# One more step ahead of the recurrence's output products, a copy moved to ScalarE, and four output stores for five

## The chip, the cores and the metric

The kernel runs on one core of one Trainium2 chip. The metric is the device time of one execution in microseconds (us). Weights, activations and output lie in the chip's HBM; one launch computes the whole layer.

## What is computed

One layer of a hybrid decoder trunk on 256 tokens of width 2048, in float32. The combined projection feeds a short convolution (branch A), a gated linear recurrence with eight heads (branch B) and two merge gates; three more projections follow.

```python
h = rmsnorm(x, norm_mix_g[i])
u = h @ w_in[i]                                  # 2048 -> 12288 columns
c_g, b_g, xa, za, q, fl, iv, og, ga, gb = jnp.split(u, split_idx, axis=-1)
ya = b_g * causal_dwconv3(c_g * xa, conv_w[i]) * jax.nn.silu(za)
# branch B, heads of 128, in chunks of the sequence:
#   a  = q . decay . k          (lower triangle of a chunk)
#   o  = (q exp b) @ state + a @ v
o = hgrn2_chunked(silu(q), kk, iv, log_f)
o = o * lax.rsqrt(jnp.mean(o * o, axis=-1, keepdims=True) + EPS)
yb = o * hg_norm_g[i] * jax.nn.silu(og)
m = jax.nn.sigmoid(ga) * (ya @ w_a_out[i]) + jax.nn.sigmoid(gb) * (yb @ w_b_out[i])
x = x + m @ w_o[i]
gate = jax.nn.sigmoid(rmsnorm(x, ple_norm_g[i]) @ w_ple_gate[i])
x = x + gate * (p[i] @ w_ple_proj[i])
return rmsnorm(x, final_norm_g)
```

## The kernel before

The 256 tokens are two tiles of 128 rows (`t` is 0 or 1). All projections run through one loop over `steps`. A step is one 256-row piece of a weight matrix by 512 columns: two row tiles `k` of 128, two token tiles `t`, and three products each, because every float32 operand is held as a rounded part and a remainder (`whi`, `wlo` for weights; `xh`, `xl` and the like for activations). So a step is twelve `L937` matmuls into two PSUM banks `g`. The order of the groups of steps is written out by hand: the projection of `p`, then for each half `j` of the recurrence and convolution columns `f, q, iv, og, c, xa, za, b` with eight steps each, then the gates with the two branch outputs, then `O` and `PG`.

Ahead of the products of a step, `split` makes the weights of the step three further on: ScalarE rounds (`L124`, `whi`), VectorE takes the remainder (`L125`, `wlo`). There are four buffers of each, so a new `whi` starts when TensorE has finished with the step four earlier. `load` asks for the raw weights further ahead still, on SyncE's DMA queue, a pair of steps in one 1 MB transfer (`L103`) into three buffers.

What belongs to a finished group of columns (its epilogue) is a Python generator. After each step, `advance` lets every active generator run to its next `yield`; so a `yield` puts what follows it one step of twelve matmuls later in the program. The engines execute their instructions in program order and wait for one another by semaphores; a scheduler may shift an instruction by a few places.

`hgrn(j)` is the generator of the recurrence for half `j` of the heads, four heads each; it runs twice, under the products of `c, xa, za, b` of the same half. With masked level products it builds the matrix `a` of 128 by 128 for each head and each token tile, and the product `bo` that links the two token tiles. Near its end stand these steps: the products `bo` (`L512`) and `bk` (`L389`); two yields; `bo` is copied from PSUM to `aoff` (`L522`), and pieces of `bk` are copied under a mask into `a[:, 0]` and `a[:, 1]` by `keep` (`L396`, eight instructions); a yield; then the twelve output products `o` (`L529`, `L530`, `L531`), each of 128 by 128 in two passes:

```python
nc.tensor.matmul(o[0][:, hs], a[:, 0, h, :], v[...], start=True, stop=True)      # L529
nc.tensor.matmul(o[1][:, hs], aoff[:, h, :], v[...], start=True, stop=False)     # L530
nc.tensor.matmul(o[1][:, hs], a[:, 1, h, :], v[...], start=False, stop=True)     # L531
```

Behind them come the squares of `o` (`L541`, ScalarE), the gate (`L547`, VectorE), the norm (`L206`, `L210`), the scaling (`L555`, ScalarE), and `turned`: four stores to DRAM (`L233`), one load back (`L235`), both on SyncE's queue, and after three more yields a transposition on VectorE (`L239`), from which `put` makes `ybT` (`L197`, `L198`). The convolution's generators run in the same stretch: `L595` and `L604` are its taps, `L264` and `L272` gates, and `ep_b` turns its own tile the same way, so its `L233` and `L235` stand in the same queue.

At the end, the last group `PG` is worked off in three parts: token tile 0, and the two halves of 256 columns of token tile 1. After each tile `last_norm(t)` gets `r`, the reciprocal root of the mean square (`L759`, `L760`), scales the 2048 columns of the tile in place and stores them. Columns 0 to 1023 are scaled by ScalarE (`L774`), 1024 to 1535 by VectorE (`L776`), 1536 to 2047 by VectorE with the gain (`L770`); each store (`L777`) goes out right after its piece is scaled, on SyncE's queue but for one on ScalarE's.

Of the kernel before, what the change touches and what calls it, by code (L numbers as in the profile page):

```python
# [11 lines left out]
AF = mybir.ActivationFunctionType  # L12
ALU = mybir.AluOpType
# [10 lines left out]
CW = 512  # L24
# [20 lines left out]
def hybrid_kernel(ctx, tc, xT, x, pT, prm, gfin, masks, w_in, w_a, w_b, w_o, w_pg, w_pp, out):  # L45
    nc = tc.nc
# [27 lines left out]
    def nm(s):  # L74
        uid[0] += 1
        return f"{s}_{uid[0]}"
# [5 lines left out]
    def bank(tag):  # L82
        return ps.tile([P, CW], F32, tag=tag, bufs=4, name=nm(tag))

    def sc(n, tag="sc", bufs=12):
        return small.tile([P, n], F32, tag=tag, bufs=bufs, name=nm(tag))
# [130 lines left out]
    def spread(ap, t):  # L217

        return ap.rearrange("p (b c t e) -> p t c b e", b=4, c=4, t=NT)[:, t]
# [120 lines left out]
    def ep_og(j, psum):  # L343
        sg, o = t4(), t4("og", 1)
        sig(psum, sg)
        times(psum, sg, o)
        state["og", j] = o
        yield
        yield from hgrn(j)

    def hgrn(j):
# [21 lines left out]
        aoff = tmp.tile([P, 4, P], F32, tag="aoff", bufs=1, name=nm("aoff"))  # L373

        def heads(ap):
            return ap.rearrange("p (h t) -> p h t", h=4)

        def quarters(B):

            n = max(B // 2, 32)  # L380
            for r in range(P // n):
                c = r ^ 1 if B >= 64 else r
                yield slice(r * n, (r + 1) * n), slice(c * n, (c + 1) * n)
# [10 lines left out]
        def keep(dst, mask, src, B):  # L394
            for r, c in quarters(B):
                nc.vector.copy_predicated(  # L396
                    out=dst[r, :, c], data=src[r, :, c],
                    mask=mask_t[r, mask : mask + 1, c].to_broadcast([r.stop - r.start, 4, c.stop - c.start]),
                )
# [24 lines left out]
        def level(B):  # L424
# [19 lines left out]
            out=y.rearrange("p (n c) -> p n c", c=SCAN), in0=b.rearrange("p (n c) -> p n c", c=SCAN),  # L444
# [11 lines left out]
        for i in range(0, len(LEVELS), 2):  # L456
# [19 lines left out]
            out=el, in0=yl,  # L476
# [12 lines left out]
            out=f.rearrange("p (n c) -> p n c", c=1), in0=br, in1=bl, op=ALU.subtract  # L489
# [8 lines left out]
        for blk in range(2):  # L498
# [4 lines left out]
                out=a[:, blk],  # L503
# [4 lines left out]
        bo = bank("s")  # L508
# [10 lines left out]
            products(bk[blk], lambda h: kk[:, h, :], lambda h: qq[:, h, :], 2)  # L519
        yield  # L520
        yield
        nc.vector.tensor_copy(out=aoff.rearrange("p h t -> p (h t)"), in_=bo)  # L522
        for blk in range(2):
            keep(a[:, blk], len(LEVELS) + 2 + blk, heads(bk[blk]), 2)
        yield
        o = [bank("s") for _ in range(2)]
        for h in range(4):
# [9 lines left out]
        for n in range(8):  # L537
            t, h = n // 4, n % 4
            if n == 4:
                yield  # L540
            nc.scalar.activation(  # L541
                out=sq[:, n * P : (n + 1) * P], in_=o[t][:, h * P : (h + 1) * P], func=AF.Square,
                scale=state["rstd1"][:, t : t + 1], accum_out=ss[:, n : n + 1],
            )
        for t in range(NT):
            s = slice(t * CW, (t + 1) * CW)
# [4 lines left out]
        for n in range(8):  # L551
            t, h = n // 4, n % 4
            if n == 4:
                yield
            nc.scalar.activation(  # L555
                out=spread(sq, t)[:, h], in_=yb[:, n * P : (n + 1) * P].rearrange("p (b e) -> p b e", e=32),
                func=AF.Identity, scale=rh[:, n : n + 1],
# [198 lines left out]
    def last_norm(t):  # L756

        xs, r, tot = state["x"], sc(1, "r3", 2), state["tot3", t]
        nc.vector.tensor_tensor(out=tot, in0=tot, in1=state["ss3"][:, t * 6 + 4 : t * 6 + 5], op=ALU.add)  # L759
        nc.gpsimd.tensor_tensor(out=r, in0=tot, in1=mhalf[:, :1], op=ALU.pow)  # L760
        n = CW // 2

        for eng, q0, q1, queue in (
            (nc.vector, 4, 5, nc.sync), (nc.vector, 5, 6, nc.sync), (nc.scalar, 0, 2, nc.sync),
            (nc.vector, 6, 8, nc.sync), (nc.scalar, 2, 4, nc.scalar),
        ):
            s = slice(q0 * n, q1 * n)
            d = xs[:, t, s]
            if q0 >= 6:
                nc.vector.scalar_tensor_tensor(  # L770
                    out=d, in0=d, scalar=r, in1=state["gfin"][:, s], op0=ALU.mult, op1=ALU.mult
                )
            elif eng is nc.scalar:
                nc.scalar.activation(out=d, in_=d, func=AF.Identity, scale=r)  # L774
            else:
                nc.vector.tensor_scalar(out=d, in0=d, scalar1=r, scalar2=None, op0=ALU.mult)  # L776
            queue.dma_start(out=out[:, t, s], in_=d)  # L777

    def ep_last(t, halves):

        last_half(t, 0, halves[0])
        sums_so_far(t)
        last_half(t, 1, halves[1])
        last_norm(t)
        yield
# [154 lines left out]
    for pos, (gi, c) in enumerate(steps[:last_group]):  # L940
# [36 lines left out]
        for i in range(2):  # L977
            k = 2 * c + i
            s = slice(i * CW, (i + 1) * CW)
# [41 lines left out]
    for t, halves in ((0, (0, 1)), (1, (0,)), (1, (1,))):  # L1021
        bk, n = bank("g"), CW // 2
        for c in range(nlast):
# [4 lines left out]
            for i in range(2):  # L1028
                k = 2 * c + i
                s = slice(i * CW + halves[0] * n, i * CW + (halves[-1] + 1) * n)  # L1030
# [5 lines left out]
        else:  # L1036
            last_half(t, halves[0], bk[:, :n])
            if halves[0] == 0:
                sums_so_far(t)
    last_norm(1)  # L1040
    finish()
    close_pool("tmp3")
# [73 lines left out]
```

## Time and profile before

| what | value |
|---|---|
| time, median of 3 runs | 831.42 us (831.42 to 831.85) |
| the profiled execution's own time | 831.84 us |
| span of the profiled execution, first to last instruction | 830.1 us |
| TensorE matmuls busy | 816.9 us (98%) |
| VectorE busy | 538.3 us (65%) |
| ScalarE busy | 430.9 us (52%) |
| DMA moved | 187.25 MB, mean 226 GB/s |
| granted TensorE clock | 0.996 |

The profile shows one execution. Times in its views are us from the start of the span. A timeline row gives the start, the duration, the engine, the source line, the operation, and the output and input tiles with their shapes; in brackets stands how long the engine sat idle before the row and what ended that. PE is the matmul, PEld the weight load that runs beside it, DVE VectorE, ACT ScalarE, POOL GpSimd, SPq the queue of SyncE and ACTq the queue of ScalarE. Matmuls are pipelined: each is recorded longer than the distance to the next one, so the rate is read from the starts. A row can hold several instructions (x8), and then its duration covers them all. The chain of waits is followed back from the last instruction, at each step to what released it.

### The profile page before, as it was taken

How to read it: one execution, taken by the hardware profiler on the slowest of the kernel's cores; microseconds unless marked ns; L12 is line 12 of the kernel's file. 1: busy time of each engine (PE TensorE's matmuls, PEld its weight loads, DVE VectorE, ACT ScalarE, POOL GpSimd, SP SyncE). 2: the span in 40 equal slices, each digit the busy share in tenths (PEclk: the TensorE clock that was granted, in tenths of full speed). 3: DMA queues.
4: the chain of work that ended last, by engine and by line, in shares of the span. 5: the costliest groups of instructions: out<-in, count | busy, mean ns of one | idle time of the engine just before them, and what ended most of it. 6: DMA issues, size and time to landing. Idle time of an engine off the chain costs nothing.

```text
span 830.1 us, 10589 instructions
## 1 busy us (share of the span) xinstructions
PE 816.9 (98%) x4122; PEld 674.3 (81%) x4122; DVE 538.3 (65%) x662; ACT 430.9 (52%) x553; POOL 84.8 (10%) x74
## 2 busy tenths in 40 slices
PE   9999999999999999999999999999999999999995
PEld 6888888878888888878888888888888888888885
DVE  6746678896866588896745545545645656679633
ACT  7666565446564465455544443443444455566522
POOL 1000035110000054100001001000100000001210
PEclk9999999999999999999999999999999999999998
DMA  9969655647876554657655755755655787987702
GB/s 341 372 256 340 222 193 197 204 153 219 277 235 232 203 203 152 204 192 241 227 203 172 254 189 196 253 203 191 231 191 198 253 281 246 330 304 269 293 0 103
DMA packets 40947, 187.25 MB, mean 226 GB/s; under 512 B 4672, under 2 KB 14400, under 8 KB 22720
## 3 DMA queue, kind: packets, MB, share of 16 engines
q1 hardware_dynamic: 40464, 185.78, 64.7%
q10 hardware_dynamic: 432, 0.79, 0.3%
q8 instruction: 32, 0.52, 0.3%
q14 instruction: 19, 0.16, 0.1%
HBM read 172.92 MB, written 13.63 MB: 225 GB/s over the span
## 4 chain that ended last, share of the span: by engine, by line
PE 93%; DVE 3%; issue 2%; ACT 1%; POOLq 0%; POOL 0%; DVEq 0%
PE g L937 91%; DVE wlo L125 1%; PE s L389 1%; PE s L937 1%; PE s L817 1%; DVE t L264 0%; PE s L531 0%; PE s L529 0%; DVE a L396 0%; ACT whi L124 0%; DVE both L396 0%; DVE X L483 0%; PE s L530 0%; DVE t L492 0%; DVE t L494 0%
## 5 line engine op out<-in xcount | busy, mean ns | idle before, releaser
L125 DVE TENSOR_TENSOR wlo<-raw,whi 128x1024 fp32r<-128x1024 f32 (+1 forms) x293 | 360.4, 1235 | 251.8 <-ACT whi L124 250.8
L124 ACT ACTIVATE whi<-raw 128x1024 fp32r<-128x1024 f32 (+1 forms) x293 | 307.6, 1056 | 323.6 <-PE g L937 279.4
L937 PE MATMUL g<-whi,xh 128*128 128x512 f32 (+1 forms) x912 | 352.0, 387 | 0.0
L937 PE MATMUL g<-whi,xl 128*128 128x512 f32 (+1 forms) x912 | 351.8, 386 | 0.0
L937 PE MATMUL g<-wlo,xh 128*128 128x512 f32 (+1 forms) x912 | 351.7, 386 | 0.0
L937 PEld LDWEIGHTS g<-whi,xh 128*128 128x128 f32 x912 | 171.3, 188 | 34.6
L937 PEld LDWEIGHTS g<-whi,xl 128*128 128x128 f32 x912 | 171.3, 188 | 34.3
L937 PEld LDWEIGHTS g<-wlo,xh 128*128 128x128 f32 x912 | 171.4, 188 | 33.9
L937 PE MATMUL g<-whi,mh 128*128 128x512 f32 x128 | 49.8, 390 | 0.0
L937 PE MATMUL g<-wlo,mh 128*128 128x512 f32 x128 | 49.7, 389 | 0.0
L937 PE MATMUL g<-whi,ml 128*128 128x512 f32 x128 | 49.6, 390 | 0.0
L659 POOL TENSOR_TENSOR t<-ga,gb 128x512 f32<-128x512 f32 x6 | 10.6, 1786 | 195.8 <-DVE gb L654 195.8
L937 PE MATMUL g<-whi,yaTh 128*128 128x512 f32 x72 | 28.3, 399 | 0.0
L937 PEld LDWEIGHTS g<-whi,mh 128*128 128x128 f32 x128 | 24.0, 188 | 5.3 <-ACT mh L665 0.3
L937 PE MATMUL g<-whi,yaTl 128*128 128x512 f32 x72 | 28.3, 396 | 0.0
L937 PEld LDWEIGHTS g<-whi,ml 128*128 128x128 f32 x128 | 23.9, 188 | 5.1 <-DVE ml L666 0.2
L937 PEld LDWEIGHTS g<-wlo,mh 128*128 128x128 f32 x128 | 24.0, 188 | 5.0
L937 PE MATMUL g<-wlo,yaTh 128*128 128x512 f32 x72 | 27.9, 390 | 0.0
L436 POOL TENSOR_TENSOR t<-b 128x512 f32<-128x512 f32 x10 | 18.9, 1890 | 67.0 <-DVE b L319 38.7
L937 PE MATMUL g<-whi,ybTh 128*128 128x512 f32 x64 | 24.9, 389 | 0.0
L937 PE MATMUL g<-whi,ybTl 128*128 128x512 f32 x64 | 24.9, 389 | 0.0
L937 PE MATMUL g<-wlo,ybTh 128*128 128x512 f32 x64 | 24.9, 389 | 0.0
(154 smaller groups left out, 522.4 us busy)
## 6 DMA issues: line engine op xcount, KB each, us to landing
raw<-in_w_in SPq DMA_DIRECT2D x93, 1024.0 KB, 5.0
raw<-in_w_o SPq DMA_DIRECT2D x16, 1024.0 KB, 5.5
raw<-in_w_pg SPq DMA_DIRECT2D x16, 1024.0 KB, 5.8
turn<-t SPq DMA_DIRECT2D x72, 128.0 KB, 2.7
t<-turn SPq DMA_DIRECT2D x18, 512.0 KB, 4.9
raw<-in_w_a SPq DMA_DIRECT2D x8, 1024.0 KB, 5.0
raw<-in_w_b SPq DMA_DIRECT2D x8, 1024.0 KB, 5.0
raw<-in_w_in SPq DMA_DIRECT2D x6, 512.0 KB, 8.3
```

The costliest lines, as they stand in the source:

```text
L124: a = nc.scalar.activation(out=hi[:, s], in_=src[:, s], func=AF.Copy)
L125: v = nc.vector.tensor_tensor(out=lo[:, s], in0=src[:, s], in1=hi[:, s].bitcast(F32), op=ALU.subtract)
L389: nc.tensor.matmul(heads(bk)[r, h, c], key(h)[:, r], query(h)[:, c], start=True, stop=True, tile_position=(0, r.start),)
L436: nc.gpsimd.tensor_tensor(out=er, in0=br, in1=ref, op=ALU.subtract)
L659: (nc.vector if j == 3 else nc.gpsimd).tensor_tensor(out=spread(m, t), in0=blocks(ga[:, s]), in1=blocks(gb[:, s]), op=ALU.add)
L817: nc.tensor.matmul(wb, warm[:, :P], warm, start=True, stop=True)
L937: nc.tensor.matmul(psum, a, b, start=first and n == 0, stop=last and n == 2)
```

## The change

In `hgrn`, `bo` is copied to `aoff` by ScalarE (an activation with the function Copy) and no longer by VectorE, and one more yield stands between the masked copies and the output products. In `last_norm`, the five pieces become four of 512 columns, in this order: 1024 to 1535 (VectorE), 0 to 511 (ScalarE), 1536 to 2047 (VectorE, with the gain), 512 to 1023 (ScalarE). Each has one store; the last of them goes out on ScalarE's queue, the other three on SyncE's.

```diff
-        nc.vector.tensor_copy(out=aoff.rearrange("p h t -> p (h t)"), in_=bo)
+        nc.scalar.activation(out=aoff.rearrange("p h t -> p (h t)"), in_=bo, func=AF.Copy)
         for blk in range(2):
             keep(a[:, blk], len(LEVELS) + 2 + blk, heads(bk[blk]), 2)
+        yield
         yield
         o = [bank("s") for _ in range(2)]
...
-        n = CW // 2
-        for eng, q0, q1, queue in (
-            (nc.vector, 4, 5, nc.sync), (nc.vector, 5, 6, nc.sync), (nc.scalar, 0, 2, nc.sync),
-            (nc.vector, 6, 8, nc.sync), (nc.scalar, 2, 4, nc.scalar),
-        ):
-            s = slice(q0 * n, q1 * n)
+        for q in (2, 0, 3, 1):
+            s = slice(q * CW, (q + 1) * CW)
             d = xs[:, t, s]
-            if q0 >= 6:
+            if q < 2:
+                nc.scalar.activation(out=d, in_=d, func=AF.Identity, scale=r)
+            elif q == 2:
+                nc.vector.tensor_scalar(out=d, in0=d, scalar1=r, scalar2=None, op0=ALU.mult)
+            else:
                 nc.vector.scalar_tensor_tensor(
                     out=d, in0=d, scalar=r, in1=state["gfin"][:, s], op0=ALU.mult, op1=ALU.mult
                 )
-            elif eng is nc.scalar:
-                nc.scalar.activation(out=d, in_=d, func=AF.Identity, scale=r)
-            else:
-                nc.vector.tensor_scalar(out=d, in0=d, scalar1=r, scalar2=None, op0=ALU.mult)
-            queue.dma_start(out=out[:, t, s], in_=d)
+            (nc.scalar if q == 1 else nc.sync).dma_start(out=out[:, t, s], in_=d)
```

In the compiled programs the order changes only near these places, and in the same way in both halves `j`. TensorE's output products stand nine `L937` matmuls later: before, they stood after the first three matmuls of a step, now behind all twelve of it. On ScalarE the copy to `aoff` stands ahead of an `L595` tap, and one more `L124` stands ahead of the squares. On VectorE the masked copies follow `L125` directly; what hangs on the output products comes about one `L125` later, and the transposition `L239` of `yb` now stands directly ahead of its four `L198`. On SyncE's queue the four `L233` of `yb` come one raw load later, and the four `L233` of `ep_b` now stand ahead of `yb`'s `L235`. In the stretch of the last rows SyncE issues six stores in place of eight.

## The prediction

> **What bounds the kernel now.** I read the page's span, busy times and chain first, then who waited on TensorE, then the chain in order of time.
>
> ```profile
> span 830.1 us, 10589 instructions
> PE 816.9 (98%) x4122; PEld 674.3 (81%) x4122; DVE 538.3 (65%) x662; ACT 430.9 (52%) x553; POOL 84.8 (10%) x74
> ...
> PE 93%; DVE 3%; issue 2%; ACT 1%; POOLq 0%; POOL 0%; DVEq 0%
> ...
> t<-turn SPq DMA_DIRECT2D x18, 512.0 KB, 4.9
> ```
>
> ```profile
> PE s L529 <- DVE a L396: 2.6, 2, 1.3
> ```
>
> ```profile
> 184.45 0.22 PE s L531 x2
> ...
> 369.06 440.21 PE g L937 x1941
> ```
>
> TensorE is the bound: 93% of the chain is its own work. Once it has work it does not stop: 1941 `L937` matmuls run in 440.21 us without a break, 0.2268 us each, so a step of twelve takes 2.72 us. In mid-kernel the views show one kind of stop: the output products `L529` wait twice for the masked copies `L396`, 2.6 us in all. The extra step works on those two stops; the new stores work on what follows the last matmul. A microsecond taken off TensorE's row ahead of 369.06 should arrive at the end whole, as nothing but TensorE's own pace stands between.
>
> **The extra step and the copy.** The timeline of TensorE at the two places, and first the entry into an earlier small product (`L512`) that waits for no other engine:
>
> ```profile
> 169.66 0.39 PE L937 MATMUL g<-whi,xl 128*128 128x512 f32 x1
> 169.98 1.09 PE L512 MATMUL s<-X 128*64 128x128 f32 x16
> ...
> 180.44 0.39 PE L937 MATMUL g<-whi,xl 128*128 128x512 f32 x1
> 182.13 0.46 PE L529 MATMUL s<-v,a 128*128 128x128 f32 x2 [1.30 <-DVE a L396]
> ...
> 182.65 0.61 PE L529 MATMUL s<-v,a 128*128 128x128 f32 x4
> 183.29 0.49 PE L531 MATMUL s<-v,a 128*128 128x128 f32 x2
> ...
> 364.12 0.39 PE L937 MATMUL g<-whi,xl 128*128 128x512 f32 x1
> ...
> 365.84 0.46 PE L529 MATMUL s<-v,a 128*128 128x128 f32 x2 [1.33 <-DVE a L396]
> ...
> 366.36 0.61 PE L529 MATMUL s<-v,a 128*128 128x128 f32 x4
> ...
> 367.00 0.49 PE L531 MATMUL s<-v,a 128*128 128x128 f32 x2
> ```
>
> The idle time in brackets (1.30 and 1.33) counts from the recorded end of a matmul, which overlaps the next; the loss is larger. Without a wait, the change from `L937` to small products costs 0.32 (169.66 to 169.98). So `L529` could have started at 180.44 + 0.32 = 180.76 and started at 182.13: 1.37 lost. Behind it the second set of masked copies stops TensorE once more: four passes at 0.11 (0.22 for two in the chain) from 182.65 end at 183.09, and `L531` starts at 183.29: 0.20. Second place: 364.44 against 365.84, 1.40; 366.80 against 367.00, 0.20. The sum is 1.57 + 1.60 = 3.17 us.
>
> The changed program puts nine more `L937` ahead, 9 x 0.2268 = 2.04 us, so the products come up at 180.76 + 2.04 = 182.80 and at 366.48, and the first `L531`, now third in each head's natural order, four passes later: 183.24 and 366.92. Is their input there? VectorE and ScalarE around both places:
>
> ```profile
> 180.18 0.69 DVE L522 COPY aoff<-s 128x512 f32<-128x512 f32 x1
> 180.78 2.46 DVE L396 COPY_PREDICATED a<-mask_t,s 32x128 f32<-32x128 int32 x8
> ...
> 183.93 2.36 DVE L125 TENSOR_TENSOR wlo<-raw,whi 128x1024 fp32r<-128x1024 f32 x2
> ...
> 363.88 0.68 DVE L522 COPY aoff<-s 128x512 f32<-128x512 f32 x1
> 364.49 2.47 DVE L396 COPY_PREDICATED a<-mask_t,s 32x128 f32<-32x128 int32 x8
> ...
> 394.01 1.23 DVE L125 TENSOR_TENSOR wlo<-raw,whi 128x1024 fp32r<-128x1024 f32 x1 [0.71 <-ACT whi L124]
> 395.16 1.24 DVE L239 STREAM_TRANSPOSE t<-t 128x1024 f32<-128x1024 f32 x1
> ```
>
> ```profile
> 175.89 1.06 ACT L124 ACTIVATE whi<-raw 128x1024 fp32r<-128x1024 f32 x1
> ...
> 180.24 1.06 ACT L124 ACTIVATE whi<-raw 128x1024 fp32r<-128x1024 f32 x1 [1.71 <-PE g L937]
> ...
> 392.92 1.06 ACT L124 ACTIVATE whi<-raw 128x1024 fp32r<-128x1024 f32 x1 [1.66 <-PE g L937]
> ```
>
> ```profile
> L700 ACT ACTIVATE t<-s 128x512 f32<-128x512 f32 x4 | 2.2, 618 | 0.0
> ```
>
> Without the copy the masked copies start at 180.18 and 363.88 and end at 182.64 and 366.35; their first half, which `L529` needs, is through 1.2 us earlier. `L531` then has 0.6 us to spare in both places. The copy itself comes on ScalarE after the `L124` at 175.89, so from 176.95, and takes about 0.62 us by `L700`, the nearest row (a plain copy of the same shape from PSUM): 177.6, five microseconds before `L530` wants it. What it pushes is one tap and one `L124`, by 0.62 us at most. The remainder of that `L124` is the first of the pair on VectorE at 183.93, and the `L124` after it (180.24) waits for TensorE for 1.71 us anyway. So I cost the moved copy at nothing. If that cover were gone, its price would be 0.62 us a place.
>
> Here a rule speaks against the edit. The Trainium skill, "ScalarE: Activation LUTs", section "Rules for kernel authors", says to use VectorE, not ScalarE, for simple operations such as add and multiply. By rows the copy is no dearer on ScalarE (0.62 against 0.68), and VectorE is what is late here. With the extra step but the copy left on VectorE, the masked copies would end as before, at 183.24 and 366.96, just at the new `L531`, and the sum would lose some 0.1 us. The rule would bring about no other outcome.
>
> What is late next? The chain behind the products (squares, gate, norm, `L555`, `L233`, `L235`, `L239`) comes a step later in the program and about 2.72 - 1.60 = 1.1 us later on the clock. It is needed only by the B projection many steps on, but it shares queues:
>
> ```profile
> 381.58 1.78 SPq L233 DMA_DIRECT2D turn<-t  x4
> ...
> 386.14 0.34 SPq L235 DMA_DIRECT2D t<-turn  x1
> 386.57 1.96 SPq L233 DMA_DIRECT2D turn<-t  x4
> ```
>
> The four stores of `yb` move from 381.58 to about 382.7 and end at 384.5. `ep_b`'s four, now directly behind them, run to 386.5. The read back needs the landing of `yb`'s stores, 2.8 us after their last issue as before (383.36 to 386.14): 387.3. With 4.9 us to landing it is there at 392.2, and the transposition `L239` now wants it at 395.16 + 1.1 = 396.3. Four microseconds to spare. Behind `L239` on VectorE the four `L198` and then `L125` are queued, on whose remainders TensorE waits in the end. There is slack there as well: a rounding starts when TensorE has finished a step and is used three steps later, 8.2 us, while its remainder is done 2.3 us after the rounding began (392.92 to 395.24). So this costs nothing. A loss would need a read over 4 + 5.9, some 10 us, late.
>
> **The last rows.**
>
> ```profile
> 823.52 0.62 DVE L776 TENSOR_SCALAR xs<-xs,r 128x256 f32<-128x256 f32 x2 [0.67 <-POOL r L760]
> 824.05 0.75 DVE L770 SCALAR_TENSOR_TENSOR xs<-xs,r,gfin_t 128x512 f32<-128x512 f32 x1
> ```
>
> ```profile
> 823.52 1.34 ACT L774 ACTIVATE xs<-xs,r 128x512 f32<-128x512 f32 x2 [2.24 <-POOL r L760]
> ```
>
> ```profile
> 823.90 0.33 SPq L777 DMA_DIRECT2D out<-xs  x1
> ```
>
> ```profile
> 825.55 0.41 SPq L777 DMA_DIRECT2D out<-xs  x1
> ```
>
> ```profile
> GB/s 0 0 0 0 0 0 0 0 82 328 241 46 138 338 384 420 348 338 379 410 348 441 369 358 266 62 20 10 0 0 0 0 0 0 0 0 0 0 0 0
> ...
> out<-xs SPq DMA_DIRECT2D x2, 256.0 KB, 3.4
> ```
>
> (The GB/s row covers 823 to 831 us in slices of 0.2.) SyncE issues its four stores from 823.90 to 825.55, and the last lands 3.4 us later, at 828.95; 1.15 us then close the span. Data flow from 824.6, break off near 825.2 (46 GB/s) and then run at about 370 GB/s to 828. Now the first store is 256 KB. Its scaling takes between 0.35 (as one half of before; the pair took 0.62) and, going up as the two-input sums do,
>
> ```profile
> L719 DVE TENSOR_TENSOR xs<-xs,t 128x512 f32<-128x512 f32 x6 | 3.9, 685 | 0.0
> ...
> L738 DVE TENSOR_TENSOR xs<-xs,t 128x256 f32<-128x256 f32 x4 | 1.6, 422 | 0.1
> ```
>
> 0.35 + 0.26 = 0.61 us, so it is issued between 823.9 and 824.16; I take the late end, as the pair's 0.62 agrees. By "VectorE: DVE Perf Modes" in the Trainium skill, section "Mode 2×_2P", a float32 product with a scalar in SBUF goes at two elements a cycle; that would put the issue some 0.1 us earlier, an estimate from the page. 256 KB last 0.7 us at that rate, so the hole closes, and 1 MB from 824.9 at 370 GB/s is out by 827.7 in place of 828.0 to 828.2: 0.3 to 0.5 us. By the issues: at the mean distance of now, (825.55 - 823.90) / 3 = 0.55 us, SyncE's third and last issue comes at 824.16 + 1.10 = 825.26, 0.3 earlier. I take 0.4. The ends are -0.2 (the later start goes through to the end and the hole stays) and +0.8. Token tile 0's stores lie under the matmuls of tile 1 and count nothing.
>
> **Sum.** 3.17 + 0.4 = 3.57 us, against the execution's own 831.84 (the span and 1.74 around it): 828.27. The median of the runs is 0.42 lower, 831.42, so 827.85; I give 827.9. Ends of this case: 2.63 by the bracketed idle time alone to 3.81 with the 0.32 counted too, and the tail's -0.2 to 0.8: 829.0 to 826.8.
>
> **Rivals.**
> *The wait stays in part.* The margin of `L531` is 0.6 us. If VectorE comes to the masked copies some 1.4 us later than now, half of each stop remains: 2 x 0.8 + 0.4 = 2.0 us, 829.4. For it: VectorE's rows at both places carry no idle time, so it is behind there. Against: what stands ahead of the copies is the same, and loses an instruction.
> *The time is given back.* VectorE's remainders or the raw loads become the next stop as TensorE comes earlier, and only the tail is left: 831.0. For it: the two remainders at 183.93 lag their roundings (the second ends at 186.29, 6.05 us after 180.24). Against: 8.2 us are allowed.
> *Slower.* `yb`'s read back, now behind `ep_b`'s stores on SyncE, comes so late that `L239` holds VectorE, and the remainders behind it stop TensorE. It decides from 10 us of lateness; at 13 us it would cost 2 x 3 - 3.57 = +2.4 us: 833.9. Against: I count about 1 us later, not 10.
> That the change does not do what it says is ruled out by the compiled order.
>
> **How the numbers follow.** Forecast 0.73, part of the wait 0.10, given back 0.09, slower 0.08. The range goes from 826.8 past the partial wait's 829.4 to 829.8 and leaves out the last two, 0.17. With 0.2% (1.66 us) as the bound, about what a measurement of this kernel can tell from no change, the first two are faster, 0.83; given back is the same, 0.09; slower 0.08.
>
> **What would show it.** Right: no wait of `L529` for `L396` on TensorE's list, the distance from `L937` into `L529` near 0.32, the masked copies straight behind `L125`, TensorE's last full run ending about 3.2 us earlier, and no hole in the GB/s row of the tail. Wrong: a new wait of `L530` on ScalarE or `L531` on VectorE, idle time of `L937` anywhere behind the products, `L239` waiting for `turn`, or SyncE's last store issued no earlier after `r` than the 2.0 us of now (823.52 to 825.55).

## The result, and the profile after

The changed kernel takes 827.37 us (median of 4 runs, 827.1 to 827.43) where the kernel before takes 831.52 beside it (831.42 to 831.85): a ratio of 0.9949, 95% interval 0.9932 to 0.9966. That is 4.15 us less; the forecast was 827.9 and the range 826.8 to 829.8. The profiled execution took 827.43 us, 4.41 less than the one of before. In the changed kernel `L937` has become `L933`, the output products `L530`, `L531`, `L532`, the stores `L773`.

The page's span, busy times and chain:

```profile
span 825.6 us, 10578 instructions
PE 815.7 (99%) x4122; PEld 674.4 (82%) x4122; DVE 536.2 (65%) x658; ACT 430.9 (52%) x555; POOL 84.7 (10%) x74
...
PE 97%; issue 1%; DVE 0%; ACT 0%; POOLq 0%; POOL 0%
```

The list of what TensorE waited for has one row left, a wait at the start that stood in the profile before as well:

```profile
PE s L813 <- DVE warm L809: 1.2, 1, 1.2
```

The chain in order of time, about its last full run of TensorE:

```profile
367.00 0.22 PE s L532 x2
367.22 438.15 PE g L933 x1932
```

That run ends at 805.37; before, it ended at 369.06 + 440.21 = 809.27. So 3.90 us of the 4.41 were gained ahead of that point (0.09 of it ahead of both places, as the first `L512` product came at 169.89 and not 169.98), and 0.51 behind it. The timeline of TensorE at the first place, entry and exit of the products, then the entry of the second:

```profile
182.39 0.39 PE L933 MATMUL g<-whi,xl 128*128 128x512 f32 x1
182.62 0.38 PE L530 MATMUL s<-v,a 128*128 128x128 f32 x2
182.84 0.39 PE L531 MATMUL s<-v,aoff 128*128 128x128 f32 x2
183.06 0.39 PE L532 MATMUL s<-v,a 128*128 128x128 f32 x2
...
185.07 0.39 PE L532 MATMUL s<-v,a 128*128 128x128 f32 x2
185.21 0.48 PE L933 MATMUL g<-whi,xh 128*128 128x512 f32 x1
...
364.15 0.39 PE L933 MATMUL g<-whi,xl 128*128 128x512 f32 x1
364.38 0.38 PE L530 MATMUL s<-v,a 128*128 128x128 f32 x2
```

No bracket is left, and the starts are evenly spaced: 0.23 from the last large matmul to the first product, 0.22 from each pair to the next. The 24 passes last from 182.62 to 185.21, 2.59 us. Before, it was 2.97 (182.13 to 185.10). Beside them on VectorE and ScalarE:

```profile
178.96 1.21 DVE L125 TENSOR_TENSOR wlo<-raw,whi 128x1024 fp32r<-128x1024 f32 x1
180.09 2.50 DVE L396 COPY_PREDICATED a<-mask_t,s 32x128 f32<-32x128 int32 x8
```

```profile
175.80 1.06 ACT L124 ACTIVATE whi<-raw 128x1024 fp32r<-128x1024 f32 x1
176.75 0.60 ACT L522 ACTIVATE aoff<-s 128x512 f32<-128x512 f32 x1
177.22 0.51 ACT L596 ACTIVATE cv<-t,prm_t 128x256 f32<-128x256 f32 x1
```

The masked copies start straight behind `L125` and end at 182.59, 0.47 us ahead of the first `L532` (183.06). The last rows, on VectorE, on SyncE's queue, and the flow of data from 819 to 827 us in slices of 0.2:

```profile
819.62 0.49 DVE L768 TENSOR_SCALAR xs<-xs,r 128x512 f32<-128x512 f32 x1 [0.67 <-POOL r L761]
```

```profile
820.13 1.30 SPq L773 DMA_DIRECT2D out<-xs  x3
```

```profile
GB/s 0 0 0 0 0 0 0 0 0 72 348 379 399 338 389 399 359 410 379 369 420 348 348 287 0 0 0 0 0 0 0 41 0 0 0 0 0 0 0 0
...
q14 instruction: 1, 0.01, 0.3%
```

The hole is gone, and data end within the slice at 823.6. The 41 GB/s at 825.2 are no store but an 8 KB fetch of instructions (q14).

### The profile page after: what moved, and what is told of

Its sections match the earlier page's. It is cut to its first block, busy times and chain, and to the rows that moved or that the text cites. A ratio compares the mean times of both kernels' runs of the same rounds, so it can differ in the third digit from the quotient of the medians.

```text
span 825.6 us, 10578 instructions
## 1 busy us (share of the span) xinstructions
PE 815.7 (99%) x4122; PEld 674.4 (82%) x4122; DVE 536.2 (65%) x658; ACT 430.9 (52%) x555; POOL 84.7 (10%) x74
## 4 chain that ended last, share of the span: by engine, by line
PE 97%; issue 1%; DVE 0%; ACT 0%; POOLq 0%; POOL 0%
PE g L933 95%; PE s L389 1%; PE s L933 1%; PE s L813 1%; PE s L512 0%; PE s L532 0%; PE s L531 0%; PE s L530 0%; ACT xs L766 0%; DVE t L736 0%; DVE t L740 0%; DVE xs L739 0%; POOLq L1107 0%; POOL r L761 0%; ACT t L735 0%
## 5 line engine op out<-in xcount | busy, mean ns | idle before, releaser
L125 DVE TENSOR_TENSOR wlo<-raw,whi 128x1024 fp32r<-128x1024 f32 (+1 forms) x293 | 360.0, 1234 | 246.0 <-ACT whi L124 245.4
L124 ACT ACTIVATE whi<-raw 128x1024 fp32r<-128x1024 f32 (+1 forms) x293 | 307.4, 1056 | 313.9 <-PE g L933 269.4
L933 PE MATMUL g<-whi,xh 128*128 128x512 f32 (+1 forms) x912 | 352.1, 387 | 0.0
L933 PE MATMUL g<-wlo,xh 128*128 128x512 f32 (+1 forms) x912 | 351.9, 386 | 0.0
L933 PE MATMUL g<-whi,xl 128*128 128x512 f32 (+1 forms) x912 | 351.8, 386 | 0.0
L933 PEld LDWEIGHTS g<-whi,xl 128*128 128x128 f32 x912 | 171.5, 188 | 34.3
L933 PEld LDWEIGHTS g<-whi,xh 128*128 128x128 f32 x912 | 171.4, 188 | 34.2
L933 PEld LDWEIGHTS g<-wlo,xh 128*128 128x128 f32 x912 | 171.5, 188 | 33.9
L933 PE MATMUL g<-whi,mh 128*128 128x512 f32 x128 | 49.8, 390 | 0.0
L933 PE MATMUL g<-wlo,mh 128*128 128x512 f32 x128 | 49.7, 390 | 0.0
L933 PE MATMUL g<-whi,ml 128*128 128x512 f32 x128 | 49.6, 390 | 0.0
L933 PEld LDWEIGHTS g<-whi,mh 128*128 128x128 f32 x128 | 24.0, 188 | 5.2 <-ACT mh L666 0.3
L933 PE MATMUL g<-whi,yaTh 128*128 128x512 f32 x72 | 28.2, 397 | 0.0
L933 PEld LDWEIGHTS g<-whi,ml 128*128 128x128 f32 x128 | 24.0, 188 | 5.1 <-DVE ml L667 0.2
L933 PEld LDWEIGHTS g<-wlo,mh 128*128 128x128 f32 x128 | 24.0, 188 | 5.0
L933 PE MATMUL g<-wlo,yaTh 128*128 128x512 f32 x72 | 28.0, 391 | 0.0
L933 PE MATMUL g<-whi,yaTl 128*128 128x512 f32 x72 | 27.9, 390 | 0.0
L933 PE MATMUL g<-whi,ybTl 128*128 128x512 f32 x64 | 24.9, 390 | 0.0
L933 PE MATMUL g<-whi,ybTh 128*128 128x512 f32 x64 | 24.9, 389 | 0.0
L933 PE MATMUL g<-wlo,ybTh 128*128 128x512 f32 x64 | 24.9, 389 | 0.0
```

Of the source, the lines that this page charges most:

```text
L124: a = nc.scalar.activation(out=hi[:, s], in_=src[:, s], func=AF.Copy)
L125: v = nc.vector.tensor_tensor(out=lo[:, s], in0=src[:, s], in1=hi[:, s].bitcast(F32), op=ALU.subtract)
L933: nc.tensor.matmul(psum, a, b, start=first and n == 0, stop=last and n == 2)
```

## The experiments

All times are medians beside runs of the kernel before on the same chip, ratios with their 95% interval. In the profiles TensorE's first long run of large matmuls begins between 17.2 and 17.7 us, long before anything that was edited; so between two profiles stretches are compared, not their ends.

**The step alone** (step_only): the extra step; the copy stays on VectorE ahead of the masked copies, and the five stores stay.

```diff
             keep(a[:, blk], len(LEVELS) + 2 + blk, heads(bk[blk]), 2)
+        yield
         yield
```

> The kernel before with the extra step alone: the copy to aoff stays on VectorE, five stores. Theory W (a stop costs what TensorE waits, 3.17 us in mid-kernel): the masked copies end as before, at about 183.24, while the third product is due 0.44 us after the first, so near 183.06 by the changed kernel's trace; a wait of about 0.2 us is left at each place. Gain 3.17 - 0.4 = 2.8 us, 828.7. Theory R (a stop costs its wait and a restart of TensorE of about 0.1 us, and the entry into the products costs nothing without a wait; 3.9 us in all): the left stops cost 0.3 each, gain 3.9 - 0.6 = 3.3 us, 828.2. If the moved copy carried the change (theory C), the gain is under 1 us.

Measured: 828.56 us (828.34 to 828.8) against 831.67, ratio 0.9962 (0.9949 to 0.9976): 3.1 us. TensorE's timeline:

```profile
182.57 0.38 PE L530 MATMUL s<-v,a 128*128 128x128 f32 x2
182.78 0.39 PE L531 MATMUL s<-v,aoff 128*128 128x128 f32 x2
183.19 0.49 PE L532 MATMUL s<-v,a 128*128 128x128 f32 x2
183.51 0.39 PE L530 MATMUL s<-v,a 128*128 128x128 f32 x2
```

The big wait is gone. `L532`, due at 183.00, comes 0.19 late, as the masked copies end late; and the pair behind it follows after 0.32, not 0.22. A stop of 0.19 costs some 0.3. The gain lies between theory W (2.8 us) and theory R (3.3); the 0.32 behind the late product is what R said.

**The copy alone** (copy_only): the copy on ScalarE, no step, five stores.

```diff
-        nc.vector.tensor_copy(out=aoff.rearrange("p h t -> p (h t)"), in_=bo)
+        nc.scalar.activation(out=aoff.rearrange("p h t -> p (h t)"), in_=bo, func=AF.Copy)
```

> The kernel before with the copy to aoff on ScalarE alone, no extra step, five stores. Theories W and R alike: the masked copies start 0.60 us earlier, the first stop at each place shrinks from 1.4 to 0.8 us, the second (0.2) stays; gain 2 x 0.6 = 1.2 us, 830.3. Theory C (VectorE's copy was what held the products): most of the mid-kernel gain, 3 us or more, 828.4.

Measured: 831.66 (11 runs), ratio 1.0001 (0.9992 to 1.0009): nothing. On VectorE the masked copies do start 0.7 us earlier (180.78 before):

```profile
180.07 2.47 DVE L396 COPY_PREDICATED a<-mask_t,s 32x128 f32<-32x128 int32 x8
```

But TensorE's list and its timeline show the wait as it was:

```profile
PE s L529 <- DVE a L396: 2.8, 2, 1.4
```

```profile
179.65 0.39 PE L937 MATMUL g<-whi,xl 128*128 128x512 f32 x1
181.43 0.46 PE L529 MATMUL s<-v,a 128*128 128x128 f32 x2 [1.40 <-DVE a L396]
```

The last large matmul stands at 179.65, not 180.44 as before. With the copy gone from VectorE the scheduler had put the products three `L937` (0.68 us) earlier in TensorE's program.

**The copy alone, the products held** (copy_held): as copy_only, with the output products called from the step loop at the place they had before, in the order they had there (`first`, `second`, `third` are the products of `L529`, `L530`, `L531`).

```diff
-        nc.vector.tensor_copy(out=aoff.rearrange("p h t -> p (h t)"), in_=bo)
+        nc.scalar.activation(out=aoff.rearrange("p h t -> p (h t)"), in_=bo, func=AF.Copy)
...
+            first(0), second(0), first(1), first(2), third(0), second(1)
+            third(1), second(2), third(2), first(3), second(3), third(3)
+
+        state["held"] = outputs
...
+                    if "held" in state:
+                        state.pop("held")()
```

> The kernel before with the copy to aoff on ScalarE, and the output products held at the place and in the order that they have in the kernel before, behind the first three large matmuls of a step. In the copy alone the products had moved to the step's start, three large matmuls (0.68 us) earlier, and the wait stayed 1.40 us. If that move ate the gain, now the wait is 0.7 to 0.8 us at each place, gain 1.2 to 1.4 us, 830.3. If the moved copy is worth nothing for another reason: 831.6.

Measured: 830.23 (11 runs), ratio 0.9983 (0.9974 to 0.9991): 1.4 us, as expected.

```profile
PE s L533 <- DVE a L396: 1.4, 2, 0.7
```

So the copy on ScalarE is worth 0.7 a place as long as the order stays. What the copy alone lost was lost to the order.

**Step and copy** (step_copy): the changed kernel with the five stores of before.

```diff
-        for q in (2, 0, 3, 1):
-            s = slice(q * CW, (q + 1) * CW)
+        n = CW // 2
+
+        for eng, q0, q1, queue in (
+            (nc.vector, 4, 5, nc.sync), (nc.vector, 5, 6, nc.sync), (nc.scalar, 0, 2, nc.sync),
+            (nc.vector, 6, 8, nc.sync), (nc.scalar, 2, 4, nc.scalar),
+        ):
+            s = slice(q0 * n, q1 * n)
...
```

> The kernel before with the extra step and the copy on ScalarE, five stores as before. Theory W: 3.17 us less, 828.3. Theory R: 3.9 us less, 827.6, no wait of TensorE on VectorE in the trace, and 0.23 us from the last large matmul to the first product. Together with the stores alone it should add up to the whole change, 4.1 to 4.5 us.

Measured: 827.92 (827.79 to 828.63), ratio 0.9956 (0.9944 to 0.9969): 3.75 us, 0.64 more than the step alone, for two stops of some 0.3 that are gone. In the profiles the stretch from the start of TensorE's first long run to the end of its last is 0.63 us shorter than with the step alone. The time again lies between theory W (828.3) and theory R (827.6); no wait is left in mid-kernel, and the way from the last large matmul to the first product is 0.23 us, as R has it.

**The price of a stop** (copy_last): with the step, the copy on VectorE, but behind the masked copies, so that it alone is late.

```diff
-        nc.vector.tensor_copy(out=aoff.rearrange("p h t -> p (h t)"), in_=bo)
         for blk in range(2):
             keep(a[:, blk], len(LEVELS) + 2 + blk, heads(bk[blk]), 2)
+        nc.vector.tensor_copy(out=aoff.rearrange("p h t -> p (h t)"), in_=bo)
+        yield
```

> The kernel before with the extra step, the copy to aoff on VectorE but behind the masked copies; five stores. The second product in each head order needs aoff, due at 182.84 by the changed kernel's trace and ready at about 183.25: a stop of 0.4 us at each place. Theory W: 0.8 us more than the step with the copy on ScalarE (827.9): 828.7. Theory R: a restart of 0.1 us on each stop besides, 828.9; the trace shows the first pass pair after the stop at 0.32 in place of 0.22.

Measured: 829.3 (829.29 to 829.39), ratio 0.9972 (0.996 to 0.9983).

```profile
182.56 0.38 PE L530 MATMUL s<-v,a 128*128 128x128 f32 x2
183.40 0.46 PE L531 MATMUL s<-v,aoff 128*128 128x128 f32 x2 [0.46 <-DVE aoff L524]
183.70 0.39 PE L532 MATMUL s<-v,a 128*128 128x128 f32 x2
```

`L531`, due at 182.78, is 0.62 late, and the next pair comes after 0.30, not 0.22: 0.70 in all for a stop whose bracket says 0.46. TensorE resumes large matmuls at 185.85, 3.29 us after its first product; in the changed kernel it was 2.59. The two places cost 1.4 us together, the difference to step_copy by median. Both theories had less (0.8 and 1.0): `aoff` was ready at 183.25 as they said, but the product started 0.15 us behind that.

**One more step** (two_steps): the changed kernel with a second extra `yield` at the same place.

```diff
         yield
         yield
+        yield
         o = [bank("s") for _ in range(2)]
```

> The changed kernel with one more step ahead of the output products (two in all beside the two of before). Theory W (after the change nothing is left to wait for at the two places, and a step of delay costs nothing by itself): TensorE enters the products as smoothly as in the changed kernel, the time is within 0.2 us of it (827.2 to 827.6). Theory D (delay of the chain behind the products has a price, since the read back and the transposition come another 2.7 us later in the shared queues): 828 to 830 us, with idle time of VectorE at the transposition or of TensorE behind it.

Measured: 827.54 (827.44 to 827.68), ratio 0.995 (0.9937 to 0.9963); within 0.2 of the changed kernel, which was compared beside other runs of before. More delay neither helps nor hurts: nothing is left to wait for there.

**The four stores alone** (tail_only): `last_norm` as changed, the rest as before.

```diff
-        for eng, q0, q1, queue in (
...
+        for q in (2, 0, 3, 1):
```

> The kernel before with the four stores alone. By the prediction's sum 0.4 us less; by the changed kernel's trace, from the start of the last scaling to the end of the span, 0.6 us less (6.6 to 6.0). 830.9 to 831.1. If the four stores gave nothing of their own and the end only shifts with TensorE: 831.5.

Measured: 831.63 (11 runs), ratio 0.9997 (0.9989 to 1.0006): hardly anything, where the prediction has 0.4 for the tail. (From the start of the last scaling to the end of the span it is 6.33 us, where before has 6.53 and copy_only, with the same five stores, 6.31.) On top of step and copy the stores are worth some 0.4 (4.15 us of gain against 3.75). SyncE's queue:

```profile
824.00 1.55 SPq L772 DMA_DIRECT2D out<-xs  x3
...
824.43 0.37 SPq L772 DMA_DIRECT2D out<-xs  x1
...
825.22 0.33 SPq L772 DMA_DIRECT2D out<-xs  x1
```

The first row covers all three stores, the other two are its second and third. The same three stores take 1.55 us here and 1.30 in the changed kernel. Two things differed in the traces: two 8 KB instruction fetches fell among the last stores, 3.00 and 4.32 us after the scaling began, and SyncE paused 0.35 us ahead of its last store.

**Fetches** (tail_pad): the four stores alone with two tiny instructions more on ScalarE, which should shift the fetches.

```diff
+        nc.scalar.activation(out=sc(8, "fill", 1), in_=mhalf, func=AF.Copy)
```

> The kernel before with the four stores alone, and two small extra ScalarE instructions of 8 columns in mid-kernel (one in each half), which nothing uses. Theory F (fetches of 8 KB of instructions fall between the last stores, where one of 16 DMA engines then carries the last bytes late; the changed kernel shows none there because its two extra ScalarE instructions move ScalarE's fetch ahead): at most one fetch between the last stores, the last landing 0.2 to 0.6 us earlier after r than the four stores alone (5.3 us), 831.1 to 831.4. If fetches do not matter: as the four stores alone, 831.6, and 5.3 us from r to the last landing.

Measured: 848.87, ratio 1.0206 (1.0192 to 1.022), 17 us slower, so the time answers nothing. (The trace has one fetch among the stores in place of two, and the last landing still 5.26 us after the scaling began.) `sc(8, "fill", 1)` is a new tile of 32 bytes a partition. The chain:

```profile
377.52 449.29 PE g L933 x1941
```

A large matmul takes 0.2315 us on average (449.29 / 1941) in place of 0.2268, at a granted clock of 0.997. By the starts in the trace it is not every one: those that read `xh`, `xl`, `mh` or `ml` come 0.233 to 0.234 apart, those that read `yaTh`, `yaTl`, `ybTh` or `ybTl` 0.227 to 0.229. The next run has the same two instructions without the new tile, and keeps the pace. So the slow pace comes with the tile; I put it down to the addresses of the tiles behind it in SBUF, which were not moved by themselves.

**The same with an existing tile** (tail_pad2), so that no address moves:

```diff
+        nc.scalar.activation(out=sc(8, "table", 1), in_=mhalf, func=AF.Copy)
```

> The four stores alone (the run tail_only), with one tiny ScalarE activation more in each half of the recurrence, which writes a small tile that exists already, so that no address in SBUF moves. Theory F (the 8 KB instruction fetches among the last stores cost the time that the four stores should have brought): ScalarE's stream is two instructions longer, as in the changed kernel, so its fetch comes ahead of the last rows; at most one fetch falls among the last stores, r to the last landing takes 4.7 to 5.1 us where tail_only had 5.3, and the time is 831.1 to 831.4. Theory N (the fetches do not matter): 5.3 us from r to the last landing and 831.6, as tail_only.

Measured: 831.5 (11 runs), ratio 0.9997 (0.9988 to 1.0006). One fetch instead of two fell among the stores, and from `r` to the last landing it still took 5.25 us (5.26 in tail_only). So the later of the two fetches was not what cost the time; the earlier one, 3.0 us after the scaling began, was still there. And that one did hold up the last bytes. The flow of data from 823 to 831 us in slices of 0.2:

```profile
GB/s 0 0 0 0 0 0 0 0 0 0 225 379 420 348 369 420 338 379 430 358 338 399 369 379 72 31 20 10 0 0 0 0 0 0 0 0 0 0 0 0
```

The full flow ends at 827.8 and a trickle runs on to 828.5, where the changed kernel's flow breaks off. A store's landing is told by sixteen updates of a semaphore. Of the last store's, fifteen come 4.42 to 4.57 us after the scaling began and one at 5.25. The fetch took 0.49 us, and the last data packets, 2 KB each, come one by one every 0.08 us: one of the sixteen DMA engines is late with its share.

**The pause.** In the twelve traces up to here (with that of tail_eight, below) SyncE pauses 0.34 to 0.36 us ahead of the 464th instruction recorded for it, whatever that is, and also ahead of the 208th, 256 earlier. The Trainium skill, "Runtime: NRT & Kernel Launch", section "Instruction fetch mechanics", says that an engine's instructions are refilled in blocks of 256 and that crossing a block is mostly hidden. The distance of 256 agrees; in the closing of the changed kernel, from the last landing to the end of the span, the pause is not hidden (0.33 us, see the part on the tail). An 8 KB fetch begins 0.6 to 1.8 us behind the end of the pause at the 464th, in all twelve; so pause and fetch come together. What stands at that place differs: before, the second of the four last stores; in tail_only the last store; in the changed kernel, whose SyncE has eight instructions fewer, an instruction of the closing, behind the landing. Two runs move it. **tail_less** is tail_only with one SyncE instruction less ahead of the last store:

```diff
-        for t in range(NT):
-            s = slice(j * CW, (j + 1) * CW)
-            nc.sync.dma_start(out=state["x"][:, t, s], in_=x[:, t, s])
+        s = slice(j * CW, (j + 1) * CW)
+
+        nc.sync.dma_start(out=state["x"][:, :, s], in_=x[:, :, s])
```

> The four stores alone, with the loads of x (L874) for both token tiles in one DMA each; by the compiled order SyncE has one instruction less in front of the last store. Theory S (the pause of 0.35 us belongs to SyncE's 464th recorded instruction): it falls behind the last store in place of ahead of it; SyncE's last issue comes about 1.45 us after r starts the scaling and not 1.77, r to the last landing takes 4.6 to 5.0 us and not 5.3, and the time is 831.2 to 831.4. Theory C: 1.77, 5.3 and 831.6 as in the run with four stores alone.

Measured: 831.23 (831.04 to 831.51, 11 runs), ratio 0.9992 (0.9983 to 1.0001), 0.58 below the runs of before beside it.

```profile
824.35 1.30 SPq L772 DMA_DIRECT2D out<-xs  x3
```

Three stores take 1.30 again. From the start of the scaling SyncE's last issue comes after 1.43 and not 1.74 us, the last landing after 4.93 and not 5.26: all as theory S had it. (Where the pause falls behind the last store, the wait for the landing covers it.) But the run moved two things, since the fetch behind the pause went with it, from 3.00 to 4.34 us after the scaling began. The landing updates of the last store tell them apart: in tail_only fourteen of sixteen come by 4.60 and the last at 5.26; here fifteen come by 4.69 and the last at 4.93. An issue 0.31 us earlier brought the bulk of the bytes no sooner; only the update that is late came sooner. So what tail_less gained fits the fetch, and not the later issue as theory S had it. The other way round, **sync_plus** gives the changed kernel two SyncE instructions more (one load of `x` in two halves), to hide the pause under the landing:

```diff
-            s = slice(j * CW, (j + 1) * CW)
-            nc.sync.dma_start(out=state["x"][:, t, s], in_=x[:, t, s])
+            n = CW // 2 if t == 0 and j in (3,) else CW
+            for s in (slice(c, c + n) for c in range(j * CW, (j + 1) * CW, n)): nc.sync.dma_start(out=state["x"][:, t, s], in_=x[:, t, s])
```

> The changed kernel with one load of x (L874, 128 by 512, token tile 0, the last of the four column groups) asked for in two halves on SyncE, some 110 us before the end; by the compiled order SyncE then has two instructions more in front of the last store. In all twelve traces so far SyncE pauses 0.34 to 0.36 us ahead of the same place of its program, its 464th recorded instruction: ahead of the last store in the run with four stores alone, between the landing and the end in the changed kernel. Theory S (the pause belongs to that place in SyncE's program): it now falls behind the last store and ahead of the long wait for the landing, which hides it; from r to the end of the span 5.6 to 5.7 us where the changed kernel had 5.99, and 827.0 to 827.15 in time. Theory C (the pause belongs to the last stores or to the closing itself): it is in the closing still, 5.9 to 6.0 us, and 827.35 to 827.5.

Measured: 827.65 (827.09 to 827.95), ratio 0.9949 (0.9936 to 0.9961), the ratio of the changed kernel: no gain. The pause was again at the 464th instruction (824.86, 0.35 us), so it belongs to that place; but the place was still behind the landing. I had taken the first wait of the closing for a short one, and it waited for the last store itself. A version that beats the changed kernel was not found.

**Eight stores** (tail_eight): the changed kernel with eight stores of 256 columns, seven on SyncE.

```diff
-        for q in (2, 0, 3, 1):
-            s = slice(q * CW, (q + 1) * CW)
+        n = CW // 2
+        for q in (4, 0, 5, 1, 6, 2, 7, 3):
+            s = slice(q * n, (q + 1) * n)
...
-            (nc.scalar if q == 1 else nc.sync).dma_start(out=out[:, t, s], in_=d)
+            (nc.scalar if q == 3 else nc.sync).dma_start(out=out[:, t, s], in_=d)
```

> The changed kernel with eight stores of 256 columns at the end, seven of them on SyncE. If the number of stores on SyncE sets the end (0.43 us each): the last is issued 3.0 us after r in place of 1.5, and the end comes 0.5 to 1.5 us later than in the changed kernel, 828.0 to 828.9. If the bytes set it (1 MB at 370 GB/s): no later than 0.2 us, 827.5.

Measured: 827.75 (827.65 to 828.01), ratio 0.9953 (0.994 to 0.9967), a gain of 3.9 us where four stores have 4.15. The last issue came 3.53 us after the scaling began (1.44 with four), the last landing 5.32 after it (4.61): 2.1 us of later issue make 0.7 of later landing, as the last SyncE store lands 1.8 us after its issue and not 3.2. The 0.25 us lie just above what the account by bytes allowed and below that by issues. (In this kernel the pause and its fetch, 1.71 us after the scaling began, stand among the early stores and not in the closing: the closing takes 1.06 us and not 1.41, so the stores themselves cost more than 0.25.)

## Why the prediction was right, and where its terms were off

**The mechanism held.** The wait of `L529` for `L396` is gone, the masked copies follow `L125` directly, TensorE runs through, and the last full run ends earlier. step_only and step_copy give 3.1 and 3.75 of the 4.15 us. None of the rivals came about: no part of the wait is left, no other wait took its place, and `yb` was no danger. The queue of SyncE:

```profile
380.68 3.85 SPq L233 DMA_DIRECT2D turn<-t  x8
384.88 0.34 SPq L235 DMA_DIRECT2D t<-turn  x1
385.26 0.44 SPq L103 DMA_DIRECT2D raw<-in_w_in  x1
387.07 0.32 SPq L235 DMA_DIRECT2D t<-turn  x1
```

```profile
393.99 1.24 DVE L239 STREAM_TRANSPOSE t<-t 128x1024 f32<-128x1024 f32 x1
```

`L239` has no bracket. One step there was wrong without consequence: the chain behind the second products was to come 1.1 us later on the clock (2.72 - 1.60). It came 0.9 earlier (380.68 against 381.58). Not a step of 2.72 but nine matmuls, 2.04, stand ahead, and the gain of both places had to be taken off, not of one. That makes some 1.8, and the squares do come 1.84 earlier (366.81 against 368.65); one `L124` and one `L125` more stand ahead of the rest of the chain, which leaves 0.9.

**Mid-kernel, forecast 3.17, measured about 3.8.** TensorE resumes at 185.10 before and at 185.21 after, with 2.04 us more of work ahead of it: 1.93, less the 0.09 from the start, 1.84 for the first place; 3.90 - 0.09 - 1.84 = 1.97 for the second. The forecast had 1.57 and 1.60. At the first place the term is short by two sizes:
- The entry without a wait was put at 0.32, from `L512`. It is 0.23, one large matmul: the 0.32 belonged to that place and not to every change to small products. 0.09.
- A stop was priced from the time the product was due to the time it started. But the pair behind a stop is late as well. In the profile of before (timeline of TensorE) these are the pairs behind the products of 182.13 and 183.29, and the large matmul with which TensorE resumes:

```profile
182.43 0.39 PE L530 MATMUL s<-v,aoff 128*128 128x128 f32 x2
...
183.62 0.39 PE L530 MATMUL s<-v,aoff 128*128 128x128 f32 x2
...
185.10 0.48 PE L937 MATMUL g<-whi,xh 128*128 128x512 f32 x1
```

0.30 and 0.33 stand where 0.22 is the pace: 0.08 + 0.11 = 0.19. copy_last and step_only show the same 0.08 and 0.10 where a stop is made at will.

1.57 + 0.09 + 0.19 = 1.85; in the same way 1.60 + 0.09 + 0.19 = 1.88 of the 1.97 at the second. The forecast's upper end of mid-kernel, 3.81, covered it only by the way: it counted the whole 0.32 into the loss, which was not the reason.

**The moved copy** was rightly costed at nothing on ScalarE (0.60 us, in a place that hides it). Its worth was put too low: "the sum would lose some 0.1 us" with the copy left on VectorE; it is 0.64 (step_only against step_copy), since each of two stops costs 0.3 with the pair behind it. The end of the masked copies was taken for "just at" the products, with no price for being 0.2 late. The Trainium skill's rule in "ScalarE: Activation LUTs", section "Rules for kernel authors", that operations such as add and multiply go to VectorE and not to ScalarE, does not name copies; taken to cover them it would have left the copy on VectorE. Here the measurement decides against it (0.60 us on ScalarE, 0.68 on VectorE, and 0.64 us of the whole time).

**The tail, forecast 0.4, measured 0.51.** The hole closed as said. The first store was issued 0.51 us after the scaling started (819.62 to 820.13), not 0.64: a scaling of 512 columns took 0.49, where I took 0.61. The estimate from "VectorE: DVE Perf Modes" in the Trainium skill, section "Mode 2×_2P" (two elements a cycle), had it 0.1 earlier, and the trace agrees: 0.49. The forecast by the issues took 0.55 us as their distance, which held SyncE's pause of 0.35; the distances were 0.43 and 0.50, and the last issue came 1.44 us after the scaling began, not 1.74.

But the account left out what the experiments found, and the 0.51 is a sum of three parts. First, the stores' own bytes land 0.31 us sooner: of the sixteen updates of the last store all but two come by 4.92 us after the scaling began before, and all by 4.61 in the changed kernel. This is the 0.3 to 0.5 that the prediction worked out. Second, the two late updates of before, at 5.13 and 5.45, are gone, as no fetch falls among the stores any more: 0.53. Third, the closing behind the last landing takes 1.41 us and not 1.08, as SyncE's pause falls into it: 0.33 lost. Four stores alone keep two fetches among the stores and give 0.04 by median; with one instruction less on SyncE they give 0.58 against their own runs of before. In the changed kernel the step has taken four instructions off SyncE, and the pause and its fetch fall behind the landing. So the mechanism of the tail was right, with 0.31 of the 0.4. That the whole came near the mark too was luck: two terms that the prediction did not have, 0.53 and -0.33, leave only 0.20 between them. For the edit by itself, by median, the forecast would have been ten times too much.

That the fetches make the late updates is read from the traces. In the thirteen traces with four or five stores, as many of the last store's sixteen updates come late, by 0.2 to 0.7 us, as fetches fall among the stores: two in before, step_only, copy_last and tail_only; one in copy_only, copy_held, step_copy, tail_pad, tail_pad2 and tail_less; none in the changed kernel, two_steps and sync_plus, where the last landing comes 4.60 to 4.63 us after the scaling began. What stays open: no run moved SyncE's fetch without its pause, and why the fetch follows the pause by 0.6 us in some kernels and by 1.7 in others was not looked into. The other fetch of before, at 3.87, is gone from the stores in each kernel with the copy on ScalarE; why it is gone in tail_less too is not known.

## What to carry to other kernels

Price a stop of TensorE from the row where it was due to the second row behind the stop, where the pace is back, and take the cost of an unhindered change of shapes from the place itself. When an edit frees an engine ahead of a wait, look where the scheduler then puts the waiting instructions: the freed time can go into an earlier start of the wait. A change of the last microseconds can depend on how many instructions stand ahead of it in a queue, since that decides where a pause and a fetch of instructions fall; so run it with the rest of the change and not only by itself, and look at the updates of the last landing one by one.

## What the runs showed of the hardware

- SyncE pauses 0.34 to 0.36 us ahead of the 208th and the 464th instruction recorded for it, whatever they are; in tail_less alone the wait for the landing covers the 464th. An 8 KB fetch begins 0.6 to 1.8 us behind the end of the pause at the 464th. In the closing the pause cost 0.33 us (1.41 and not 1.08); ahead of the last store it delayed the issue by 0.3 us, but not the bulk of the landing updates.
- TensorE's pace comes back only one pair after a stop: 0.30 to 0.33 us from the first pair to the second, where 0.22 is usual.
- With one tile of 32 bytes a partition more in SBUF, 1941 matmuls of 128x512 took 0.2315 us each on average and not 0.2268, at the same granted clock: 0.233 to 0.234 where they read `xh`, `xl`, `mh` or `ml`, and no more than 0.229 where they read `yaT` or `ybT` tiles. That the tiles' addresses make it is not shown.
- A fetch of instructions is one packet of 8 KB in a queue of its own, and took 0.31 to 2.1 us. In the thirteen traces with four or five last stores, each fetch among them went with one of the last store's sixteen landing updates that came 0.2 to 0.7 us late.
